# A prefix block of gated linear attention, Mamba-2 and PEER on one core: the opening products queued half a round earlier, a shorter look-ahead of the weight stream, and one step more in the first attention head

## The chip, the cores and the metric

The kernel runs on one core of one Trainium2 chip. The metric is device microseconds of one launch, from the first to the last instruction with what little lies around it; lower is better.

## The reference

One layer of a hybrid backbone. 256 latent tokens and 256 context tokens (512 columns together) of width D = 2048 pass through an RMSNorm that is modulated by the conditioning vector, one wide input projection that feeds gated linear attention (GLA, 4 heads) and a Mamba-2 state-space mixer, merge gates, an output projection, and then a second modulated norm and product-key experts (PEER).

```python
# modulation: six vectors of D for the latent tokens (from c) and for the context tokens (from c_ctx)
h = rmsnorm(x, w) * (1 + scale) + shift              # the same for ctx
q, k, v, r, lr_f, lr_b, z, xbc, dt_f, dt_b, gl = split(h @ w_in)
g_f = log_sigmoid(lr_f @ w_lr2_f + b_lr_f) / 16      # log decays of GLA, and g_b from lr_b
# GLA, a head: qd = q exp(b), kd = k exp(-b); o = tril(qd kd^T) v + qd s; both directions
...
# Mamba-2 SSD, merge gates, output projection, gated residual; then norm, PEER experts, gated residual
```

## The kernel before

All products are float32 to nearly full precision: each operand is split into a high and a low part, and a product is three matmuls (high by high, high by low, low by high). So every 512 KB chunk of weights (a tile `raw`, 128 x 1024) is split before TensorE uses it: ScalarE (ACT) copies it to `hi` (line 49), and VectorE (DVE) subtracts to get `lo` (line 50). The class `Stream` holds the list of chunks, loads them on SyncE's queue (line 42, three buffers `raw`) and splits them (four buffers each of `hi` and `lo`). `get()` hands the next chunk to the products, and first calls `ahead()`, which issues loads up to `loads` chunks ahead and splits up to `splits` ahead. Instructions run on each engine in the order in which the code issues them.

The same SyncE queue carries the weights of the modulation, called rides (line 64, 512 KB each, tiles `raw0` and `s4`, seven slots in the opening). Two rides feed one piece: `ada_piece` (line 263, tile `ad`, eight short matmuls in the trace). A ride's slot comes free when the piece has run on TensorE that used the ride seven before it. A load `raw` that has to wait for its buffer holds up the rides behind it in the queue.

The opening computes the modulated input `Hhi`, `Hlo` pair by pair of 128-row tiles, and the products that can begin with a part of it. A list `START`, written out by a loop over rounds, sets the order. A round has four pieces; after the fourth the sums stand in `ad`, and `ada_out` copies them (ACT, line 269), turns them (TensorE, line 274, `sc<-sel,s`) and adds the bias (DVE, line 279, `mods`). `h_pair` (lines 309 to 321) then makes one pair: DVE scales (line 314), ACT rounds to `Hhi` (line 316), DVE subtracts to `Hlo` (line 318), and DVE prepares the next pair (line 321). Each pair feeds two products `v` (`v_part`, lines 336 to 338, 12 matmuls into four banks `mm`) and two products `ld` (lines 426 to 428, 6 matmuls into banks `sc`); in the later rounds a whole product `k` follows (lines 328 to 330, 24 matmuls, a bank `sc`). There are 32 pieces, 8 turnings, 16 `v`, 16 `ld` and 4 `k` in the opening.

After it come the units, one weight tile after another (lines 328 to 330, banks `mm`), with the decays (`dt_stage` from line 665, `decay` lines 482 to 500) and the attention heads as generators beside them: at each `tick`, once per weight chunk, a generator runs up to its next `yield`. `gla(hd)` takes the exponentials of a head (`exps`, lines 534 to 550), multiplies (`prods`, lines 555 to 561) and multiplies on TensorE (`diag`, line 568).

The lines that the change touches are `START` and what reads it, `Stream._load` and `Stream._split`, the tag of the copy in `ada_out`, and two yields in `gla`.

Of the kernel before, what the change touches and what calls it, by code (L numbers as in the profile page):

```python
# [10 lines left out]
F32 = mybir.dt.float32  # L11
F32R = mybir.dt.float32r
# [7 lines left out]
P = 128  # L20
# [8 lines left out]
class Stream:  # L29
# [8 lines left out]
        self.rides, self.aboard, self.nr = [], deque(), 0  # L38

    def _load(self, i):  # L40
        t = self.pool.tile([P, 1024], F32, name="raw", tag="raw", bufs=self.loads - self.splits)
        self.nc.sync.dma_start(t, self.plan[i])
        self.raw[i] = t

    def _split(self, i):
        t = self.raw.pop(i)
        hi = self.pool.tile([P, 1024], F32R, name="hi", tag="hi", bufs=self.splits + 1)
        lo = self.pool.tile([P, 1024], F32R, name="lo", tag="lo", bufs=self.splits + 1)
        self.nc.scalar.activation(hi, t, AF.Copy)  # L49
        self.nc.vector.tensor_sub(lo, t, hi.bitcast(F32))  # L50
        self.done[i] = (hi, lo)
# [43 lines left out]
def hybrid_block_kernel(ctx, tc, A, out):  # L95
    nc = tc.nc
# [4 lines left out]
    streams = ctx.enter_context(tc.tile_pool(name="streams", bufs=1))  # L101
    dram = ctx.enter_context(tc.tile_pool(name="dram", bufs=1, space=DRAM))
    psum = ctx.enter_context(tc.tile_pool(name="psum", bufs=1, space=PSUM))
    st = Stream(nc, streams, 6, 3)

    def mmbank(shape=(P, 512)):
        return psum.tile(list(shape), F32, name="mm", tag="mm", bufs=4)
# [42 lines left out]

    START = []
    for c in range(10):
        todo = [("v", c - 2, 0), ("ld", c - 2, 0), ("v", c - 2, 1), ("ld", c - 2, 1)] if c > 1 else []
        if 4 < c < 9:
            todo.append(("k", c - 5, 0))
        for i in range(8):
            if c < 8 and i % 2:
                START.append(("ada", c, i // 2))  # L160
                if not c:
                    START.append(("norm", i // 2, 0))
            if i == 3 and 0 < c < 9:
                START.append(("h", c - 1, 0))
            if todo:
                START.append(todo.pop(0))

    plan = []
    for k, a, b in START:
        if k == "ada":  # L170
# [39 lines left out]
    w4 = es_w.enter_context(tc.tile_pool(name="w4", bufs=1, reuse_waits="tile"))  # L210
    es_x = ExitStack()
    xp = es_x.enter_context(tc.tile_pool(name="xp", bufs=1))
# [46 lines left out]
    def ada_piece(i, raws=None):  # L259

        raws = [r.rearrange("p (k n) -> p k n", k=2) for r in (raws or st.alight())]
        for g in range(4):
            mm_(adb[32 * g:32 * g + 32, :], cS[:, 4 * i + g, :], raws[g // 2][:, g % 2, :], start=i == 0, stop=i == 3,  # L263
                tile_position=(0, 32 * g), skip_group_check=True)
# [26 lines left out]
    def norm1():  # L291
        pst = scbank()
        for i in range(4):
            sq = [xp.tile([P, 512], F32, name="sq1", tag="sq1", bufs=3) for _ in range(2)]
            for j in range(4):
                nc.scalar.activation(sq[min(j, 1)], xc[:, 4 * i + j], AF.Square)
                if j:
                    nc.vector.tensor_add(sq[0], sq[0], sq[1])
            mm_(pst, ones, sq[0], start=i == 0, stop=i == 3)
            if i != 1:  # L300
                yield
        nc.scalar.activation(rs1, pst, AF.Ln, bias=eps, scale=1.0 / D)
        nc.scalar.activation(rs1, rs1, AF.Exp, scale=-0.5)
        nc.vector.tensor_mul(xc[:, 0:2], xc[:, 0:2], rs1[:, None, :].to_broadcast([P, 2, 512]))
        yield
# [37 lines left out]
    bg, later, ended = [], [], set()  # L343
# [3 lines left out]
    def step():  # L347
        todo = later[:]
        later.clear()
        for g in list(bg):  # L350
            if next(g, "end") == "end":
                bg.remove(g)
        for f in todo:
            f()
# [38 lines left out]
    XT, CT = slice(0, 256), slice(0, 512)  # L393
    pv0 = [mmbank() for _ in range(4)]
    n1 = norm1()
    ada_sb = lambda: w4.tile([P, 512], F32, name="s4", tag="s4", bufs=5)
    plr = pdt = None
    Kt = {a: w4.tile([P, 2, 512], F32, name="s4", tag="s4", bufs=5) for a in range(2)}
    for k, a, b in START:
        if k == "ada":  # L400
            ada_piece(b)
            if st.nr < start_rides:
                st.board()
            if b == 3:
                bg.append(ada_out(a))
        elif k == "norm":
            next(n1)
            if a == 3:
                st.ahead()
        elif k == "h":  # L410
            while ("ada", a) not in ended:
                step()
            h_pair(a)
        elif k == "v":
            if b == 0:
                wv = v_weights()
            v_part(pv0, wv, 2 * a + b, b)
        elif k == "ld":
            kt = 2 * a + b
            if kt == 0:  # L420
                plr, pdt = scbank(), scbank()
            if kt % 4 == 0:
                ld = [w.rearrange("p (w k f) -> p w k f", w=2, f=P) for w in st.get()]
            for w, pp in enumerate((plr, pdt)):
                Whi, Wlo = (t[:, w, kt % 4] for t in ld)
                mm_(pp, Whi, Hhi[:, kt, CT], start=kt == 0, stop=False)
                mm_(pp, Whi, Hlo[:, kt, CT], start=False, stop=False)
                mm_(pp, Wlo, Hhi[:, kt, CT], start=False, stop=kt == KT - 1)
        else:
            pk = scbank()  # L430
            mm3(pk, st.get(), 0, 8, Hhi, Hlo, CT, True, True)
            later.append(lambda a=a, pk=pk: nc.scalar.activation(Kt[a // 2][:, a % 2], pk, AF.Copy))
        step()
    es_x.close()
    wk = es_w.enter_context(tc.tile_pool(name="wk", bufs=1, reuse_waits="tile"))
    st.limit = st.side = None
    SZ = {"s1": 256, "s2": 512, "s4": 1024}
    NBUF = {"s1": 10, "s2": 22, "s4": 5}

    def wt(tag, shape, dtype=F32):  # L440
        assert int(np.prod(shape[1:])) <= SZ[tag]
        return (w4 if tag == "s4" else wk).tile(list(shape), dtype, name=tag, tag=tag, bufs=NBUF[tag])
# [79 lines left out]
    def gla(hd):  # L522
# [40 lines left out]
        def diag(d):  # L563
            qd, kd = E[d][1:3]
            for n in range(2):
                s = slice(n * P, n * P + P)
                for k in range(2):
                    mm_(P1[:, 2 * d + n], kd[:, k, s], qd[:, k, s], start=k == 0, stop=k == 1)
# [3 lines left out]
        prods(0)  # L572
        yield from exps(1)
        yield
        diag(0)
        prods(1)
        yield
        yield
        diag(1)
        P2 = scbank((P, 2, P))  # L580
        for d in range(2):
# [505 lines left out]
    for i in range(8):  # L1087
# [4 lines left out]
        t = mp.tile([P, 2, T], F32, name="ma", tag="mx", bufs=8)  # L1092
# [3 lines left out]
    for i in range(8):  # L1096
# [3 lines left out]
        t = op.tile([P, 2, 256], F32, name="mt", tag="mt", bufs=2)  # L1100
# [36 lines left out]
    for i in range(8):  # L1137
# [7 lines left out]
        for e in range(2):  # L1145
            k = 2 * i + e
# [198 lines left out]
    ada_sb = lambda: kp.tile([P, 512], F32, name="o2", tag="o2", bufs=3)  # L1345
    pq = {}
    for j, e, h in QORD:
        if j < 2:
            pq.setdefault((j, e), mmbank((P, 256)) if h == 0 else None)
        elif e == 0 and h == 0:  # L1350
            t = mmbank((P, 2, 256))
# [119 lines left out]
    for b in range(NB):  # L1471
# [4 lines left out]
        for group in ([0], [1], [2], [3]) if b < NB - 1 else ([0], [1], [2, 3]):  # L1476
# [7 lines left out]
            for order in ([(t, i, j) for i in group for j in range(2) for t in range(2)] if len(group) == 1 else  # L1484
                          [(t, i, j) for t in range(2) for i in group for j in range(2)]):
                t, i, j = order
# [96 lines left out]
```

## Time and profile before

| what | value |
|---|---|
| median of 3 runs | 3626.37 us (3626.19 to 3629.07) |
| profiled execution | 3628.86 us, span 3627.1 us |
| mean granted TensorE clock | 0.993 |
| TensorE matmul busy | 3546.5 us, 98% |
| VectorE, ScalarE, GpSimd busy | 65%, 46%, 10% |
| chain that ended last | PE 92%, DVE 4%, DMA 2%, ACT 1% |

The profiled execution lies 1.76 us above its span, and within the range of the three runs, 2.5 us above their median. TensorE is busy nearly all the time and makes up nearly all of the chain, so what is left to change is the 80 us in which it is not busy, and the stretches in which its clock is granted at the lower level.

### The profile page before, as it was taken

Reading aid. Unit: us, or ns where it says so; the run is one execution under the profiler, and the core shown is the slowest. Engines: PE = TensorE matmul, PEld = TensorE weight load, DVE = VectorE, ACT = ScalarE, POOL = GpSimd, SP = SyncE. Lnnn points to the kernel's source line nnn. Section 1 sums busy time; section 2 is a strip of 40 time slices with the busy share of each in tenths; the row PEclk is TensorE's granted clock in tenths of the full one; section 3 lists DMA queues with packets and bytes.
Section 4 is the critical chain, followed back from the end, with each engine's and each line's share of the span. In section 5 each row is a group of like instructions: output and inputs, shape, how many; then the busy total and the mean of one; then the engine's idle time right before and its main releaser. Section 6 shows DMA issues by size and latency. Waiting matters only on the chain.

```text
span 3627.1 us, 58908 instructions
## 1 busy us (share of the span) xinstructions
PE 3546.5 (98%) x23679; PEld 3186.4 (88%) x23679; DVE 2368.4 (65%) x3569; ACT 1665.6 (46%) x2225; POOL 370.6 (10%) x424
## 2 busy tenths in 40 slices
PE   5989999999999999999998999999999999999998
PEld 2688899988888888999998999999999999998886
DVE  3375565777878777655545787875555555556777
ACT  2254444445555555654433446464444444444344
POOL 0000000000000000110002016360000000000004
PEclk8999999999999999999999999999999999999999
DMA  8644555655665565567666557677666666666774
GB/s 304 230 140 142 172 170 179 208 170 189 210 206 184 176 191 174 167 230 245 193 209 218 172 182 203 195 208 221 198 198 197 198 197 198 198 198 206 240 228 144
DMA packets 214145, 715.39 MB, mean 197 GB/s; under 512 B 24688, under 2 KB 24832, under 8 KB 213360
## 3 DMA queue, kind: packets, MB, share of 16 engines
q1 hardware_dynamic: 188928, 625.04, 53.5%
q0 software_dynamic: 24944, 86.59, 8.7%
q8 instruction: 186, 3.05, 0.3%
q14 instruction: 87, 0.71, 0.1%
HBM read 679.93 MB, written 31.60 MB: 196 GB/s over the span
## 4 chain that ended last, share of the span: by engine, by line
PE 92%; DVE 4%; DMA 2%; ACT 1%; issue 1%; POOL 0%; DVEq 0%; SPq 0%; ACTq 0%; POOLq 0%
PE mm L328 20%; PE mm L330 20%; PE mm L329 19%; PE mm L1498 6%; PE mm L1497 6%; PE mm L1499 6%; PE mm L336 2%; PE sc L1304 2%; PE mm L337 2%; PE mm L338 2%; DVE lo L50 1%; PE sc L875 1%; PE ad L263 1%; PE sc L615 1%; PE sc L808 1%
## 5 line engine op out<-in xcount | busy, mean ns | idle before, releaser
L50 DVE TENSOR_TENSOR lo<-raw,hi 128x1024 fp32r<-128x1024 f32 x996 | 1234.3, 1246 | 1011.8 <-ACT hi L49 1003.5
L49 ACT ACTIVATE hi<-raw 128x1024 fp32r<-128x1024 f32 x996 | 1046.0, 1058 | 1383.5 <-PE mm L329 624.5
L328 PE MATMUL mm<-Hhi,hi 128*128 128x256 f32 (+1 forms) x2272 | 737.6, 325 | 1.4 <-ACT hi L49 1.4
L330 PE MATMUL mm<-Hhi,lo 128*128 128x256 f32 (+1 forms) x2272 | 724.7, 319 | 4.0 <-DVE lo L50 4.0
L329 PE MATMUL mm<-Hlo,hi 128*128 128x256 f32 (+1 forms) x2272 | 724.2, 319 | 0.0
L328 PE MATMUL mm<-h2hi,hi 128*128 128x256 f32 x2304 | 657.7, 285 | 0.0
L329 PE MATMUL mm<-h2lo,hi 128*128 128x256 f32 x2304 | 653.1, 283 | 2.5 <-DVE h2lo L1175 2.5
L330 PE MATMUL mm<-h2hi,lo 128*128 128x256 f32 x2304 | 652.6, 283 | 0.0
L328 PEld LDWEIGHTS mm<-Hhi,hi 128*128 128x128 f32 x2272 | 435.4, 192 | 37.0 <-issue 5.3
L330 PEld LDWEIGHTS mm<-Hhi,lo 128*128 128x128 f32 x2272 | 435.2, 192 | 34.4 <-DVE lo L50 5.0
L329 PEld LDWEIGHTS mm<-Hlo,hi 128*128 128x128 f32 x2272 | 435.7, 192 | 30.3 <-issue 1.9
L329 PEld LDWEIGHTS mm<-h2lo,hi 128*128 128x128 f32 x2304 | 442.4, 192 | 6.2 <-DVE h2lo L1175 3.1
L328 PEld LDWEIGHTS mm<-h2hi,hi 128*128 128x128 f32 x2304 | 442.1, 192 | 4.1 <-ACT h2hi L1172 0.8
L330 PEld LDWEIGHTS mm<-h2hi,lo 128*128 128x128 f32 x2304 | 442.1, 192 | 0.0
L1498 PE MATMUL mm<-lo,ph 128*128 128x512 f32 x1024 | 406.1, 397 | 5.7 <-DVE lo L50 5.7
L1497 PE MATMUL mm<-hi,ph 128*128 128x512 f32 x1024 | 406.5, 397 | 0.0
L1499 PE MATMUL mm<-hi,pl 128*128 128x512 f32 x1024 | 405.1, 396 | 0.0
L1498 PEld LDWEIGHTS mm<-lo,ph 128*128 128x128 f32 x1024 | 193.0, 188 | 49.5 <-DVE lo L50 7.2
L1499 PEld LDWEIGHTS mm<-hi,pl 128*128 128x128 f32 x1024 | 193.1, 189 | 46.3
L1497 PEld LDWEIGHTS mm<-hi,ph 128*128 128x128 f32 x1024 | 193.2, 189 | 42.8
L330 PE MATMUL mm<-yh,lo 128*128 128x256 f32 x768 | 217.3, 283 | 1.0 <-DVE lo L50 1.0
L328 PE MATMUL mm<-yh,hi 128*128 128x256 f32 x768 | 217.1, 283 | 0.0
(337 smaller groups left out, 4556.1 us busy)
## 6 DMA issues: line engine op xcount, KB each, us to landing
raw<-in_w_f_dram SPq DMA_DIRECT2D x288, 512.0 KB, 3.7
raw<-in_u_dram SPq DMA_DIRECT2D x256, 512.0 KB, 4.1
raw<-in_v_dram SPq DMA_DIRECT2D x256, 512.0 KB, 4.1
ride<-in_w_ada_dram SPq DMA_DIRECT2D x240, 256.0 KB, 3.9
raw<-in_w_so_dram SPq DMA_DIRECT2D x64, 512.0 KB, 4.2
raw<-in_w_ada_dram SPq DMA_DIRECT2D x45, 512.0 KB, 7.3
raw<-in_w_v_dram SPq DMA_DIRECT2D x32, 512.0 KB, 3.6
s<-cum_d POOLq DMA_DIRECT2D x64, 256.0 KB, 6.1
```

Of the source, the lines that this page charges most:

```text
L49: self.nc.scalar.activation(hi, t, AF.Copy)
L50: self.nc.vector.tensor_sub(lo, t, hi.bitcast(F32))
L328: mm_(ps, Whi[:, j, :], hi[:, k, tok], start=start and j == 0, stop=False)
L329: mm_(ps, Whi[:, j, :], lo[:, k, tok], start=False, stop=False)
L330: mm_(ps, Wlo[:, j, :], hi[:, k, tok], start=False, stop=stop and j == n - 1)
L336: mm_(pv[tb], Hhi[:, k, tok], Whi[:, j, :], start=k == 0, stop=False)
L337: mm_(pv[tb], Hhi[:, k, tok], Wlo[:, j, :], start=False, stop=False)
L338: mm_(pv[tb], Hlo[:, k, tok], Whi[:, j, :], start=False, stop=k == KT - 1)
L1304: mm_(pg[:, j], o1[:, j], o2[:, j], start=True, stop=True)
L1497: mm_(ps[t, i], ghi, Whi, start=j == 0 and k == 0, stop=False)
L1498: mm_(ps[t, i], ghi, Wlo, start=False, stop=False)
L1499: mm_(ps[t, i], glo, Whi, start=False, stop=j == 1 and k == 1)
```

## The change

Five edits, all in the first 280 us of the program.

1. `START`: a round has four slots instead of eight. The pair of round c - 1 is made right behind the first piece of round c, as before, but its products are queued from the third slot of the same round (before: from the first slot of the next round). Products stand one between two pieces, two where more than four are queued; what is left is put at the end, so that the last item is the last `k`.
2. `Stream(nc, streams, 5, 2)` in place of 6, 3 for the opening: loads run five chunks ahead and splits two. The numbers of buffers (three `raw`, four `hi` and `lo`), which were worked out from these two, are now written as they were. After the opening the look-ahead is set to 6, 3.
3. The copy of the sums takes a buffer `sq1` (three, used before that by the norm) instead of `s4`, a tag it shared with rides and the tiles of `k`.
4. After a `k` the loop goes on without a `step()`, and its copy (line 432) is issued behind the next item.
5. `gla(0)` yields once more ahead of `diag(0)` and once more ahead of `diag(1)`.

No instruction is added or removed on any engine; only the order changes, and in it only the opening and `gla(0)`.

```diff
     def _load(self, i):
-        t = self.pool.tile([P, 1024], F32, name="raw", tag="raw", bufs=self.loads - self.splits)
+        t = self.pool.tile([P, 1024], F32, name="raw", tag="raw", bufs=3)
...
-        hi = self.pool.tile([P, 1024], F32R, name="hi", tag="hi", bufs=self.splits + 1)
-        lo = self.pool.tile([P, 1024], F32R, name="lo", tag="lo", bufs=self.splits + 1)
+        hi = self.pool.tile([P, 1024], F32R, name="hi", tag="hi", bufs=4)
+        lo = self.pool.tile([P, 1024], F32R, name="lo", tag="lo", bufs=4)
...
-    st = Stream(nc, streams, 6, 3)
+    st = Stream(nc, streams, 5, 2)
...
-    START = []
+    START, todo = [], []
     for c in range(10):
-        todo = [("v", c - 2, 0), ("ld", c - 2, 0), ("v", c - 2, 1), ("ld", c - 2, 1)] if c > 1 else []
-        if 4 < c < 9:
-            todo.append(("k", c - 5, 0))
-        for i in range(8):
-            if c < 8 and i % 2:
-                START.append(("ada", c, i // 2))
-                if not c:
-                    START.append(("norm", i // 2, 0))
-            if i == 3 and 0 < c < 9:
+        for i in range(4):
+            if c < 8:
+                START.append(("ada", c, i))
+            if c == 0:
+                START.append(("norm", i, 0))
+            if i == 0 and 0 < c < 9:
                 START.append(("h", c - 1, 0))
-            if todo:
-                START.append(todo.pop(0))
+            if i == 2 and 0 < c < 9:
+                todo += [("v", c - 1, 0), ("ld", c - 1, 0), ("v", c - 1, 1), ("ld", c - 1, 1)]
+                if c > 4:
+                    todo.append(("k", c - 5, 0))
+            for _ in range(2 if len(todo) > 4 else 1):
+                if todo:
+                    START.append(todo.pop(0))
+    START += todo
...
-    ada_sb = lambda: w4.tile([P, 512], F32, name="s4", tag="s4", bufs=5)
+    ada_sb = lambda: xp.tile([P, 512], F32, name="sq1", tag="sq1", bufs=3)
...
             later.append(lambda a=a, pk=pk: nc.scalar.activation(Kt[a // 2][:, a % 2], pk, AF.Copy))
+            continue
+        while later:
+            later.pop(0)()
         step()
...
+    st.loads, st.splits = 6, 3
...
         yield from exps(1)
         yield
+        if hd == 0:
+            yield
         diag(0)
         prods(1)
         yield
         yield
+        if hd == 0:
+            yield
         diag(1)
```

TensorE around the first product, before. `ad` takes pieces (the last row that begins with `s4_` is the piece of two rides that were the first behind three loads), `mm` takes the first `v`:

```order
L263 MATMUL ad_147<-raw0_225,cS_143 32x512 x2
L263 MATMUL ad_147<-raw0_227,cS_143 32x512 x2
L263 MATMUL ad_147<-s4_256,cS_143 32x512 x2
L263 MATMUL ad_147<-s4_258,cS_143 32x512 x2
L336 MATMUL mm_150<-hi_240,Hhi_71 128x512
L337 MATMUL mm_150<-lo_241,Hhi_71 128x512
```

And after the change, the same place:

```order
L266 MATMUL ad_147<-raw0_225,cS_143 32x512 x2
L266 MATMUL ad_147<-raw0_227,cS_143 32x512 x2
L339 MATMUL mm_150<-hi_238,Hhi_71 128x512
...
L341 MATMUL mm_153<-hi_238,Hlo_72 128x512
L266 MATMUL ad_147<-s4_250,cS_143 32x512 x2
L266 MATMUL ad_147<-s4_252,cS_143 32x512 x2
L429 MATMUL sc_314<-Hhi_71,hi_242 128x512
...
L431 MATMUL sc_315<-Hhi_71,lo_243 128x512
L266 MATMUL ad_147<-raw0_274,cS_143 32x512 x2
L266 MATMUL ad_147<-raw0_276,cS_143 32x512 x2
L277 MATMUL sc_336<-sel2_108,sq1_312 128x2 x4
```

The first `v` (12 matmuls) now stands ahead of the piece that uses `s4_250` and `s4_252`, and one `ld` stands between that piece and the next.

VectorE between the norm and the first pair, before:

```order
L304 TENSOR_TENSOR xc_79<-xc_79,rs1_149 128x1024
L50 TENSOR_TENSOR lo_241<-raw_98,hi_240 128x1024
L50 TENSOR_TENSOR lo_245<-raw_100,hi_244 128x1024
L50 TENSOR_TENSOR lo_249<-raw_102,hi_248 128x1024
L279 TENSOR_TENSOR mods_142<-sc_260,b_ada_118 128x2x2x2
```

and after:

```order
L307 TENSOR_TENSOR xc_79<-xc_79,rs1_149 128x1024
L50 TENSOR_TENSOR lo_239<-raw_98,hi_238 128x1024
L50 TENSOR_TENSOR lo_243<-raw_100,hi_242 128x1024
L282 TENSOR_TENSOR mods_142<-sc_254,b_ada_118 128x2x2x2
```

One split fewer stands ahead of the first pair. On SyncE's queue the loads and rides of the same stretch stood, before, so:

```order
L42 DMA raw_234<-in_w_v_dram 128x1024
L42 DMA raw_236<-in_w_ld_dram 128x1024
L42 DMA raw_238<-in_w_v_dram 128x1024
L64 DMA s4_256<-in_w_ada0_dram 128x1024
L64 DMA s4_258<-in_w_ada0_dram 128x1024
```

and stand so after:

```order
L42 DMA raw_234<-in_w_v_dram 128x1024
L42 DMA raw_236<-in_w_ld_dram 128x1024
L64 DMA s4_250<-in_w_ada0_dram 128x1024
L64 DMA s4_252<-in_w_ada0_dram 128x1024
```

One load has left its place ahead of the two rides. In the first attention head TensorE went, before, from the last matmul of one chunk of a unit to `diag(0)` (line 568):

```order
L330 MATMUL mm_1671<-Hhi_71,lo_1572 128x256
L568 MATMUL sc_1556<-s2_1561,s2_1562 128x128 x4
L328 MATMUL mm_1671<-Hhi_71,hi_1624 128x256
```

and goes after (`diag` is now line 575):

```order
L333 MATMUL mm_1671<-Hhi_71,lo_1572 128x256
L331 MATMUL mm_1671<-Hhi_71,hi_1624 128x256
...
L333 MATMUL mm_1671<-Hhi_71,lo_1625 128x256
L575 MATMUL sc_1556<-s2_1561,s2_1562 128x128 x4
L331 MATMUL mm_1671<-Hhi_71,hi_1674 128x256
```

One chunk of 24 matmuls has moved ahead of `diag(0)`.

## Rows read from the trace of the kernel before

**Rows 1.** The page's busy times: us, share of the span, instructions.

```profile
PE 3546.5 (98%) x23679; PEld 3186.4 (88%) x23679; DVE 2368.4 (65%) x3569; ACT 1665.6 (46%) x2225; POOL 370.6 (10%) x424
```

**Rows 2.** Busy time of each engine in four stretches (us from the start): length, then PE, PEld, DVE, ACT, POOL busy with instructions, the granted TensorE clock, the DMA engines' share, GB/s.

```profile
20.00:30.00 10.00, 7.31 (x26) 1.42 (x22) 3.46 (x5) 4.20 (x8) 0.00 (x0) 0.93 1.03 420
40.00:90.00 50.00, 35.95 (x161) 18.36 (x162) 17.90 (x32) 8.05 (x13) 0.00 (x0) 0.83 0.75 276
94.70:185.60 90.90, 90.68 (x455) 61.88 (x454) 31.94 (x56) 22.40 (x31) 0.54 (x1) 1.00 0.57 211
196.00:235.00 39.00, 34.61 (x214) 31.71 (x214) 37.80 (x71) 18.95 (x28) 1.08 (x2) 0.94 0.38 97
```

**Rows 3.** TensorE in order of time, 38 to 95 us: start, duration, line, operation, and in brackets the idle time before it and what ended that.

```profile
38.06 1.93 PE L263 MATMUL ad<-raw,cS 128*32 128x512 f32 x16
48.88 3.13 PE L263 MATMUL ad<-s,cS 128*32 128x512 f32 x8 [8.90 <-DMA s<-in_w_ada_dram]
51.94 0.73 PE L336 MATMUL mm<-hi,Hhi 128*128 128x512 f32 x1
55.14 1.07 PE L263 MATMUL ad<-raw,cS 128*32 128x512 f32 x8
56.13 1.05 PE L274 MATMUL sc<-sel,s 128*128 128x2 f32 x8
57.05 0.48 PE L426 MATMUL sc<-Hhi,hi 128*128 128x512 f32 x1
...
73.10 0.63 PE L427 MATMUL sc<-Hlo,hi 128*128 128x512 f32 x1
73.53 0.63 PE L428 MATMUL sc<-Hhi,lo 128*128 128x512 f32 x1
...
86.13 1.51 PE L263 MATMUL ad<-raw,cS 128*32 128x512 f32 x4 [3.84 <-DMA raw<-in_w_ada_dram]
...
93.81 1.05 PE L274 MATMUL sc<-sel,s 128*128 128x2 f32 x8
```

**Rows 4.** SyncE's queue in order of time, 41 to 82 us: start, duration of the issues, line, tile from tensor.

```profile
41.95 0.33 SPq L42 DMA_DIRECT2D raw<-in_w_v_dram  x1
42.34 0.90 SPq L64 DMA_DIRECT2D s<-in_w_ada_dram  x2
...
56.34 0.39 SPq L64 DMA_DIRECT2D raw<-in_w_ada_dram  x1
63.81 0.33 SPq L42 DMA_DIRECT2D raw<-in_w_v_dram  x1
...
66.15 0.98 SPq L64 DMA_DIRECT2D s<-in_w_ada_dram  x2
81.07 0.33 SPq L42 DMA_DIRECT2D raw<-in_w_ld_dram  x1
```

**Rows 5.** Waits of SyncE's queue from 0 to 200 us: the waiting line, what released it, us in total, times, the longest.

```profile
SPq L42 <- DVE lo L50: 59.3, 12, 20.5
```

**Rows 6.** VectorE in order of time, 38 to 64 us.

```profile
38.44 3.49 DVE L50 TENSOR_TENSOR lo<-raw,hi 128x1024 fp32r<-128x1024 f32 x3
41.85 0.16 DVE L279 TENSOR_TENSOR mods<-sc,b_ada 128x8 f32<-128x8 f32 x1
...
43.67 1.34 DVE L318 TENSOR_TENSOR Hlo<-xc,Hhi 128x512 fp32r<-128x512 f32 x2
...
62.56 1.23 DVE L50 TENSOR_TENSOR lo<-raw,hi 128x1024 fp32r<-128x1024 f32 x1 [7.70 <-ACT hi L49]
63.70 0.16 DVE L279 TENSOR_TENSOR mods<-sc,b_ada 128x8 f32<-128x8 f32 x1
```

**Rows 7.** ScalarE in order of time, two rows between 43 and 80 us.

```profile
43.01 1.28 ACT L316 ACTIVATE Hhi<-xc 128x512 fp32r<-128x512 f32 x2 [2.90 <-DVE xc L314]
...
78.73 1.06 ACT L49 ACTIVATE hi<-raw 128x1024 fp32r<-128x1024 f32 x1 [12.10 <-PE mm L338]
```

**Rows 8.** TensorE where nothing waits, 172 to 182 us: the first matmul of a `k`, of the `v` after it, of the `ld` after that, and of the next `v`.

```profile
172.00 0.39 PE L328 MATMUL sc<-Hhi,hi 128*128 128x512 f32 x1
...
177.44 0.39 PE L336 MATMUL mm<-hi,Hhi 128*128 128x512 f32 x1
...
180.16 0.39 PE L426 MATMUL sc<-Hhi,hi 128*128 128x512 f32 x1
...
181.52 0.39 PE L336 MATMUL mm<-hi,Hhi 128*128 128x512 f32 x1
```

**Rows 9.** TensorE in order of time from the first unit to the first head's `diag`, 185 to 261 us.

```profile
185.60 0.39 PE L328 MATMUL mm<-Hhi,hi 128*128 128x512 f32 x1
...
201.94 0.50 PE L492 MATMUL sc<-lrS,s 128*128 128x512 f32 x1 [1.73 <-DVE s L487]
...
233.06 0.39 PE L330 MATMUL mm<-Hhi,lo 128*128 128x256 f32 x1 [2.18 <-DVE lo L50]
...
250.74 2.05 PE L568 MATMUL sc<-s,s 128*128 128x128 f32 x8 [3.78 <-DVE s L558]
...
259.79 1.13 PE L568 MATMUL sc<-s,s 128*128 128x128 f32 x8 [0.74 <-DVE s L558]
```

**Rows 10.** VectorE in order of time, 246 to 251 us.

```profile
246.96 1.23 DVE L50 TENSOR_TENSOR lo<-raw,hi 128x1024 fp32r<-128x1024 f32 x1 [3.71 <-PE mm L330]
...
249.90 0.69 DVE L558 TENSOR_TENSOR s<-s,s 128x512 f32<-128x512 f32 x1
```

## The prediction

> **What bounds the kernel now.** I read the page's busy times first, then the busy times by stretch, then the rows of each engine in the two stretches that the change touches. TensorE is busy for 98% of the span [rows 1], so a gain can come only from where it is not, or from where its clock is low. From 40 to 90 us it is busy for 35.95 of 50 us at a mean granted clock of 0.83; from 94.7 to 185.6 us it is busy for 90.68 of 90.9 us at 1.00 [rows 2]. The opening's loss thus lies almost all ahead of 95 us.
>
> To price that loss I put together what the opening would take with no wait. Undisturbed, a piece takes 0.99 us (55.14 to 56.13) and a turning of the sums 0.92 (56.13 to 57.05) [rows 3]; a `k` takes 5.44 us (172.00 to 177.44), a `v` 2.72 (to 180.16) and an `ld` 1.36 (to 181.52) [rows 8]. The pieces that start at 38.06 end at 39.99 [rows 3], and the first unit starts at 185.60 [rows 9], 145.6 us later. Between lie 25 pieces (24.8), 7 turnings (6.4), 16 `v` (43.5), 16 `ld` (21.8) and 4 `k` (21.8), 118.3 us. So 27.3 us are lost. Up to the end of the fourth turning (93.81 + 0.92 = 94.7 [rows 3]) there are 10 pieces, 3 turnings, 5 `v` and 4 `ld`, 31.7 us of work in 54.7 us: 23.0 us are lost there. The other 4.3 us come after it, where TensorE shows no idle time. They are the small delays where one kind of product follows another: the first `ld` matmul takes 0.48 us where the ones of a row take 0.39 [rows 3, 8].
>
> What makes the 23.0 us: TensorE waits 8.90 us for the first ride that stands behind three loads in SyncE's queue, runs that piece in 3.13 us in place of 0.99, and later waits 3.84 us for another ride; the matmuls around 73 us come 0.43 us apart where 2.72 us for a `v`'s twelve are 0.23, the lower of the clock's two levels, after the idle time ahead of them [rows 3]. Why the rides are late is seen on the queue. It stands still from 56.7 to 63.81 and from 67.1 to 81.07 us, each time in front of a load `raw` [rows 4], and such loads wait 59.3 us in all for the subtraction that frees their buffer [rows 5]. The subtraction waits for the copy `hi`, and that copy waited 12.10 us for a `v` on TensorE, the last reader of the `hi` buffer it was to fill [rows 7]. So the loop is: look-ahead of three splits with four buffers makes ScalarE wait for the product that runs, the load behind it waits, the rides behind the load wait, and TensorE waits for the rides.
>
> **The change part by part.** No instruction is added or removed; each term is a wait.
>
> *Look-ahead 5, 2.* With the same four buffers, a split goes into a buffer whose reader ended one chunk earlier, so the copy has no wait for the product that runs. This takes away the 12.10 us kind of wait on ScalarE and the two gaps in the queue, 7.1 and 14 us. It also takes one load out of its place ahead of the rides (41.95, [rows 4]) and one of three subtractions out of its place ahead of the first pair (38.44 for 3.49 us, so 1.15 us [rows 6]). What it costs: weights are split one chunk later. The cover is one chunk's product; between two chunks lie at least a `v` or `ld` and a piece, 2.35 us, against a copy (1.06) and a subtraction (1.23) in a row, 2.29 us [rows 6, 7], and mostly far more. I cost it at nothing.
>
> *Order of the products.* The first pair's `mods` come at 41.85, and its `Hhi` is whole at 43.01 + 1.28 = 44.3 [rows 6, 7]; 1.15 us earlier this is 43.1, the first of the two tiles about 42.5. In the new order the first `v` then runs while the ride for the next piece comes, instead of behind it. It starts cold: 12 matmuls at 0.43 are 5.2 us, to 47.7. The ride was issued at 42.34 [rows 4] and used at 48.88 [rows 3], 6.5 us; now it is issued about 41.2 with one transfer of 512 KB (0.524 MB at the 0.42 MB/us of 20 to 30 us [rows 2], 1.25 us) fewer ahead, so it lands by 46.5 to 47.7. The piece and that `v`, which ended at 55.1 before, end about 49.3: 5.8 us gained here. The work to there is 3.7 us of the 9.3 since 39.99, so 5.6 us stay lost.
>
> From there to the fourth turning the queue must bring 20 rides and 4 loads, 24 transfers or 12.6 MB, in the 39.7 to 80 us that a full TensorE gives them; a round needs 10 transfers, 5.2 MB, in 4 pieces, a turning, two `v` and two `ld`, 13.0 us. At the 420 GB/s of 20 to 30 us [rows 2] that is 12.5 us: just enough, so I leave 1.5 us of loss for it. The Trainium skill ("DMA: Bandwidth & Descriptors", section "Where 436 GB/s comes from") says that for transfers from HBM to SBUF the HBM side, about 358 GB/s, binds. By that a round would take 14.6 us, 1.6 us more than TensorE needs, some 6 us over four rounds, and the opening would gain 9 instead of the sum below; the 420 GB/s over ten microseconds of this trace speak against it.
>
> More changes of kind between products, two or so in a round, at 0.1 us each way as above: 1 us over the eight rounds gets worse. So the opening keeps 5.6 + 1.5 + 4.3 + 1.0 = 12.4 us of its 27.3 and gains 15. The bounds are 10 (one more wait like the 3.84 stays, with its slow matmuls) and 20 (the first `v` runs warm, the transfers never limit).
>
> *The tag of the sums' copy, the later copy of `k`.* The copy no longer waits for a ride's slot or a `k` tile. It must end ahead of the next piece, which now comes one `ld` (1.36 us) behind instead of one `v` (2.72); the copy has half the columns of a split's 1.06 us [rows 7], so some 0.5 us, and ScalarE is free then. Nothing; at worst, with a split (1.06) just ahead of it, 0.3 us in a round, 2.4.
>
> *The end of the opening.* The last `k` now stands between the last `v` and the first unit, so 5.44 us of TensorE's work lie over the emptying of the `v` banks and the first splits. In the units' first 40 us VectorE is busy 37.80 of 39.0 us [rows 2], and TensorE waits 1.73 us and 2.18 us for it [rows 9]. VectorE's work starts about 5 us earlier relative to TensorE's. Bounds: 0, as a full VectorE gives no time back, and the 3.9 of these two waits and some slow matmuls behind them, 6. I take 2.6.
>
> *`gla(0)`.* `diag(0)` waits 3.78 us for the multiplications, which end at 249.90 + 0.69 = 250.6 behind a subtraction that ended at 248.2; the matmuls after it are slow (2.05 us for eight, against 1.13 later) [rows 9, 10]. One chunk of 24 matmuls, 2.9 us, moves into the wait. Its `lo` is the subtraction that ended at 248.2, so it starts 1.2 us late. That leaves about 1.2 us of the 3.78, and takes away a part of the slow stretch (1 us). I take 3, bounds 0 (the same wait ahead of the chunk instead) and 5. The 0.74 of the second `diag` is left out.
>
> **The sum.** 15 + 2.6 + 3 = 20.6 us. From the profiled execution's 3628.9 that is 3608.3 us. That execution lies 2.5 us above the median of the runs shown, and the result will be a median, so I predict 3606.
>
> **The rivals.**
>
> *Only the opening gains.* VectorE, full from 196 to 235 us [rows 2], takes the end's gain back, and the chunk ahead of `diag(0)` waits for its own `lo` as long as `diag` waited. For it speaks that both are behind the same engine; against it, that in `gla(0)` the subtraction ended 2.4 us ahead of the products. 3626.4 - 15 = 3611.
>
> *The transfers bind.* If the queue delivers as from 40 to 90 us before, 276 GB/s [rows 2], the 12.6 MB take 45.6 us, so the fourth turning comes 5 us later than with 420, and the next round 19 in place of 13 us, 6 more. Of 15 us 4 are left; with 3 of the rest, 3619. Against it: those 276 hold two gaps of 7 and 14 us in which the queue itself waited for a buffer [rows 4].
>
> *Slower.* The cover of a pair got shorter. Between a turning and the first product of its pair stood an `ld`, `v`, `ld` and three pieces, 8.4 us; now a `v`, an `ld` and two pieces, 6.1 us. The pair itself takes 3.2 us (41.85 to 45.0 [rows 6]). Its bias add stood once 6.6 us behind its turning (57.05 to 63.70), since a subtraction that waited for its copy was ahead of it [rows 3, 6]. If that comes back in each round, a pair is 9.8 us behind, 3.7 us too late, with eight slow matmuls behind each (1.6 us): 7 times 5.3 is 37 us and the time 3643. It decides against the change from 2.9 us a round. Against it: the copy no longer waits for the product that runs, and so the subtraction doesn't.
>
> *The change doesn't do what it says.* The first ride stays as late and the queue finds another reason to wait: no more than the 5 of the first `v`, 3622 to 3626.
>
> **How the numbers follow.** Forecast (3602 to 3611) 0.50; more than that, down to 3597, 0.10; only the opening 0.15; transfers 0.13; no effect 0.07; slower 0.05. A change of 0.2%, 7.25 us, can be told from none: faster is below 3619.1, slower above 3633.6. Faster: 0.50 + 0.10 + 0.15 and half of the transfers, 0.82; slower 0.05; the rest 0.13. The range 3597 to 3619 leaves out no effect, slower, and the far half of the transfers, 0.18.
>
> **What would show it.** Right: the first `v` near 42.5 us and ahead of the piece; no gap over 5 us on SyncE's queue in front of a load between 50 and 90 us; no wait of `hi` on a `v` of 10 us; the fourth turning near 80 us and the first unit near 171; the wait ahead of `diag(0)` near 1 us. Wrong: TensorE waits for `Hhi` or `Hlo` in each round (the slower case), or for rides all through 50 to 90 us with the queue never standing still (transfers); or the first unit near 171 but the time at 3611 (only the opening).

## The result

The changed kernel takes 3605.99 us (median of 5 runs, 3605.44 to 3607.89) against 3626.19 (5 runs); the ratio is 0.9944, 95% interval 0.9932 to 0.9956. It is faster by 20 us, as forecast. The profiled executions lie further apart: their spans differ by 22.1 us, since the one before lies 2.7 us above its median. The changed kernel's profiled execution took 3606.86 us, with a span of 3605.0.

The page's busy times after, which answer to [rows 1]:

```profile
PE 3542.9 (98%) x23679; PEld 3183.0 (88%) x23679; DVE 2367.0 (66%) x3569; ACT 1666.1 (46%) x2225; POOL 372.0 (10%) x424
```

TensorE does the same matmuls, in 3.6 us less of busy time (the mean granted clock is 0.995 against 0.993); the other 18.5 us of the two spans were idle time. By stretch, to be read beside [rows 2]:

```profile
40.00:50.00 10.00, 7.47 (x24) 4.30 (x25) 5.74 (x11) 3.00 (x5) 0.00 (x0) 0.83 0.94 337
50.00:60.00 10.00, 10.00 (x58) 5.61 (x57) 6.55 (x11) 3.07 (x4) 0.00 (x0) 1.00 1.02 417
60.00:70.00 10.00, 10.00 (x59) 6.02 (x58) 3.11 (x9) 2.18 (x4) 0.00 (x0) 1.00 1.03 419
70.00:80.00 10.00, 10.00 (x59) 5.07 (x51) 3.38 (x3) 2.29 (x3) 0.00 (x0) 1.00 0.96 372
80.00:172.00 92.00, 92.00 (x465) 62.80 (x465) 38.05 (x65) 26.50 (x37) 0.54 (x1) 1.00 0.66 233
```

From 50 to 172 us TensorE is full at a granted clock of 1.00; its idle time in the opening, and its low clock, now lie from 40 to 50. TensorE in order of time there, with the first turning ahead of it, the fourth turning, and the first matmul of the first unit (compare [rows 3]):

```profile
36.78 1.05 PE L277 MATMUL sc<-sel,sq 128*128 128x2 f32 x8
37.77 1.92 PE L266 MATMUL ad<-raw,cS 128*32 128x512 f32 x16
42.27 0.79 PE L339 MATMUL mm<-hi,Hhi 128*128 128x512 f32 x1 [2.57 <-ACT Hhi L319]
...
46.87 1.05 PE L266 MATMUL ad<-s,cS 128*32 128x512 f32 x4
48.10 1.05 PE L266 MATMUL ad<-s,cS 128*32 128x512 f32 x4 [0.19 <-DMA s<-in_w_ada_dram]
49.09 0.50 PE L429 MATMUL sc<-Hhi,hi 128*128 128x512 f32 x1
...
51.67 1.05 PE L277 MATMUL sc<-sel,sq 128*128 128x2 f32 x8
...
79.67 1.05 PE L277 MATMUL sc<-sel,sq 128*128 128x2 f32 x8
...
169.40 0.39 PE L331 MATMUL mm<-Hhi,hi 128*128 128x512 f32 x1
```

The first turning stood in the kernel before at

```profile
37.07 1.05 PE L274 MATMUL sc<-sel,s 128*128 128x2 f32 x8
```

The first `v` runs at 42.27 while the ride comes, and the piece ends at 49.1. SyncE's queue in the same stretch (compare [rows 4]):

```profile
40.53 0.33 SPq L42 DMA_DIRECT2D raw<-in_w_ld_dram  x1
40.91 0.90 SPq L64 DMA_DIRECT2D s<-in_w_ada_dram  x2
...
52.03 0.33 SPq L42 DMA_DIRECT2D raw<-in_w_v_dram  x1
...
52.93 6.60 SPq L64 DMA_DIRECT2D raw<-in_w_ada_dram  x5
59.62 0.38 SPq L42 DMA_DIRECT2D raw<-in_w_ld_dram  x1
```

The two standstills of 7 and 14 us are gone. Up to 180 us the copy `hi` waited for a `v` like this before, and like this after (us in total, times, the longest):

```profile
ACT hi L49 <- PE mm L338: 37.9, 4, 12.1
```

```profile
ACT hi L49 <- PE mm L341: 1.9, 4, 0.5
```

The queue's loads, though, wait as long for the subtraction as in [rows 5] (59.3 us up to 200 us):

```profile
SPq L42 <- DVE lo L50: 63.7, 17, 10.8
```

So that total is no measure of the loss. Between 50 and 90 us no load holds the queue longer than the 4.8 us ahead of 52.03, and TensorE waits for no ride there.

Then the units. The first starts at 169.40 us, 16.2 earlier than in [rows 9]; rows from there to the next unit `v`, of which the last row is the seventh matmul, the first that waits for ScalarE to empty a bank:

```profile
183.15 0.43 PE L499 MATMUL sc<-lrS,s 128*128 128x512 f32 x1
...
208.89 0.38 PE L333 MATMUL mm<-Hhi,lo 128*128 128x256 f32 x1 [1.97 <-DVE lo L50]
...
214.20 0.39 PE L333 MATMUL mm<-Hhi,lo 128*128 128x256 f32 x1 [0.70 <-DVE lo L50]
...
228.20 0.39 PE L331 MATMUL mm<-Hhi,hi 128*128 128x256 f32 x1 [0.77 <-ACT hi L49]
229.46 0.39 PE L333 MATMUL mm<-Hhi,lo 128*128 128x256 f32 x1 [0.76 <-DVE lo L50]
233.69 1.05 PE L575 MATMUL sc<-s,s 128*128 128x128 f32 x8
...
258.01 0.50 PE L339 MATMUL mm<-hi,Hhi 128*128 128x512 f32 x1 [1.20 <-ACT s L981]
```

The first decay product no longer waits, nor does `diag(0)` (line 575); in its place two waits of 0.77 and 0.76 us stand at the chunk ahead of it. The two waits for `lo` near 209 and 214 us, 2.67 together, answer to waits of 0.48 (at 227.75) and 2.18 (at 233.06) before, so nothing was gained at these two. The row that answers to the last one stood in the kernel before at

```profile
279.84 0.51 PE L336 MATMUL mm<-hi,Hhi 128*128 128x512 f32 x1 [1.56 <-ACT s L970]
```

From the first unit to this row it took 94.2 us before and 88.6 after, 5.6 less. With the 16.2 of the opening that is 21.8 of the 22.1 us between the two spans; what comes later is as long as before.

### The profile page after: what moved, and what is told of

Same layout as the page of the kernel before. It is cut to its first block, busy times and chain, and to the rows that moved or that the text cites. A ratio compares the mean times of both kernels' runs of the same rounds, so it can differ in the third digit from the quotient of the medians.

```text
span 3605.0 us, 58893 instructions
## 1 busy us (share of the span) xinstructions
PE 3542.9 (98%) x23679; PEld 3183.0 (88%) x23679; DVE 2367.0 (66%) x3569; ACT 1666.1 (46%) x2225; POOL 372.0 (10%) x424
## 4 chain that ended last, share of the span: by engine, by line
PE 91%; DVE 4%; DMA 3%; ACT 1%; issue 1%; SPq 0%; DVEq 0%; POOL 0%; ACTq 0%; POOLq 0%
PE mm L331 19%; PE mm L332 19%; PE mm L333 19%; PE mm L1508 6%; PE mm L1509 6%; PE mm L1510 6%; PE mm L339 2%; PE sc L1315 2%; PE mm L340 2%; PE mm L341 2%; DVE lo L50 1%; PE sc L886 1%; PE ad L266 1%; PE sc L626 1%; PE sc L819 1%
```

## The experiments

All times are medians. Two measures of the trace tell more than the whole time: the first unit's start, and the time from there to the row of the `v` above, called the head below. What lies ahead of the second turning differs between executions: the first turning starts at 35.1 to 37.5 us, and in the five profiled executions that have the changed kernel's order and look-ahead up to there the second follows 14.6 to 16.9 us behind it. From the second turning to the first unit these five take 117.69 to 117.73 us. The opening of before was profiled twice, in the kernel before and with the yields alone, and took 148.5 and 145.8 us from the first turning to the first unit; from 70 to 80 us the granted clock was 0.83 in the one and 1.00 in the other.

**Look-ahead alone.** On the kernel before:

```diff
-    st = Stream(nc, streams, 6, 3)
+    st = Stream(nc, streams, 5, 2)
...
+    st.loads, st.splits = 6, 3
```

(with the buffers kept at three and four, and the second line behind the opening.)

> The kernel before with one edit: in the opening loads run five chunks ahead and splits two, with the same three and four buffers; order of the products, tag and attention as before. Theory (two halves: the look-ahead frees the queue, the order fills the first wait): the queue's two standstills in front of a load (7 and 14 us) and the 12 us wait of the copy hi on a v are gone, one load fewer stands ahead of the first ride, so the first wait shrinks from 8.9 to about 6.5 us and the 3.84 us wait and the slow matmuls after it go; of the 23.0 us lost up to the fourth turning about 11 stay, the fourth turning ends near 83 us in place of 94.7, the time is 3614 to 3617. Rival 1 (the order is all of it): the rides come as late as before, the fourth turning ends at 92 to 95, the time is 3622 to 3626. Rival 2 (the look-ahead is all of it): the same gain as the whole opening, the first unit starts near 169.5 to 171, the time is 3609 to 3611.

3612.8 us against 3627.8, ratio 0.9966 (0.9951 to 0.998). TensorE in order of time, and the waits of `hi` up to 180 us:

```profile
35.11 1.05 PE L274 MATMUL sc<-sel,s 128*128 128x2 f32 x8
...
46.09 3.17 PE L263 MATMUL ad<-s,cS 128*32 128x512 f32 x8 [7.98 <-DMA s<-in_w_ada_dram]
...
80.63 1.05 PE L274 MATMUL sc<-sel,s 128*128 128x2 f32 x8
...
170.23 0.39 PE L328 MATMUL mm<-Hhi,hi 128*128 128x512 f32 x1
...
186.78 0.50 PE L493 MATMUL sc<-lrS,s 128*128 128x512 f32 x1 [1.91 <-DVE s L488]
...
235.40 2.05 PE L569 MATMUL sc<-s,s 128*128 128x128 f32 x8 [4.54 <-DVE s L559]
```

```profile
ACT hi L49 <- PE mm L338: 5.4, 3, 1.8
```

The first wait is hardly smaller, and yet the fourth turning stands at 80.6 and the first unit at 170.2, 15.4 us earlier than before. Of these, 2.0 are an earlier first turning, within the scatter of that turning. From the first turning to the first unit it takes 135.1 us, against 148.5 before and 132.6 in the changed kernel: 13.4 of 15.9. The theory's half and half is wrong: in the opening the look-ahead is most of it, as rival 2 said, though the time lies 2 us above that rival's range. The waits of the units and the first head are as before.

**Look-ahead short at the first only.** The kernel of the last experiment, with the look-ahead of before set again at the first `v`:

```diff
+                if (a, b) == (0, 0):
+                    st.loads, st.splits = 6, 3
```

> The kernel before with the look-ahead of five and two only up to the first v, and of six and three from there on; order, tag and attention as before. One load fewer stands ahead of the first late ride and one subtraction fewer ahead of the first pair, as in the look-ahead alone; but from the first v on the copy hi again goes into the buffer whose reader is running. Theory (most of the look-ahead's 15 us comes from the copy that no longer waits for a running product, and so from the queue that no longer stands still): the standstills of 7 and 14 us are back, TensorE waits for rides again by the third or fourth turning, which ends near 91 us, the first unit starts at 181 to 185, and the time is 3622 to 3626. Rival (the one load and the one subtraction are it): the fourth turning ends at 81 to 84, the first unit starts at 170 to 174, and the time is 3611 to 3615.

3625.3 us, ratio 0.9999 (0.999 to 1.0008). SyncE's queue and TensorE:

```profile
55.82 0.33 SPq L64 DMA_DIRECT2D raw<-in_w_ada_dram  x1
63.43 0.33 SPq L42 DMA_DIRECT2D raw<-in_w_v_dram  x1
...
65.80 1.08 SPq L64 DMA_DIRECT2D s<-in_w_ada_dram  x2
78.85 0.33 SPq L42 DMA_DIRECT2D raw<-in_w_ld_dram  x1
```

```profile
83.72 3.62 PE L263 MATMUL ad<-raw,cS 128*32 128x512 f32 x8 [3.72 <-DMA raw<-in_w_ada_dram]
...
91.28 1.05 PE L274 MATMUL sc<-sel,s 128*128 128x2 f32 x8
```

The queue stands still for 7.3 and 12.0 us again, the copy `hi` waits 26.0 us for three `v` (the longest 9.9), the 3.7 us wait is back, the first unit starts at 183.6. So the gain comes from the copy that no longer waits for a running product, not from the one load and subtraction that left the front.

**Products half a round later.** The changed kernel, its products queued at the start of the next round:

```diff
-            if i == 2 and 0 < c < 9:
-                todo += [("v", c - 1, 0), ("ld", c - 1, 0), ("v", c - 1, 1), ("ld", c - 1, 1)]
-                if c > 4:
+            if i == 0 and 1 < c:
+                todo += [("v", c - 2, 0), ("ld", c - 2, 0), ("v", c - 2, 1), ("ld", c - 2, 1)]
+                if 4 < c < 9:
```

> The changed kernel with its products queued as before at the start of the next round (first v behind the second turning), all else as changed: round of four slots, look-ahead five and two, tag, attention. Theory (the first v fills the wait for the first ride): TensorE waits again for that ride, 7 to 8 us idle from 39.7 us with a cold piece behind it, and all later rounds run full; the first unit starts 4 to 6 us later than in the changed kernel (169.4), the time is 3610 to 3612. Rival (the queue sets the pace, so what TensorE does first doesn't matter): the first unit starts within 1 us of 169.4 and the time stays at 3606.

3616.1 us, ratio 0.9971 (0.9961 to 0.9981), the first unit at 178.7, 9.3 us later than in the changed kernel, where 4 to 6 were expected, and the time is 4 us above the theory's. One row of TensorE, and the busy times of a stretch:

```profile
46.85 3.16 PE L266 MATMUL ad<-s,cS 128*32 128x512 f32 x8 [8.03 <-DMA s<-in_w_ada_dram]
```

```profile
50.00:60.00 10.00, 9.30 (x39) 5.62 (x38) 5.40 (x11) 3.75 (x5) 0.00 (x0) 0.61 0.68 272
```

The wait of 8 us is back, and the clock, 0.61 in this stretch, stays low until near 58 us, inside the first `v`. That `v` starts at 54.30, behind the second turning, where in the kernel before it stood ahead of it: this list is later than the old one, so its loss overstates what the new list gains over the old. It also puts the last `k` back ahead of the last `v`, which adds to its head (92.5 us). So early queueing is worth at least the wait within the new rounds; beside the old list it is worth far less, since the look-ahead alone starts its units 8.5 us earlier than this kernel.

**The yields**, taken out of the changed kernel, and put alone into the kernel before:

```diff
-        if hd == 0:
-            yield
         diag(0)
...
-        if hd == 0:
-            yield
         diag(1)
```

> The changed kernel without the two added yields in the first attention head. Theory: the wait of 3.8 us in front of the first diag is back, with slow matmuls behind it; measured from the first unit's start (169.4) to the first v of the next unit, 88.6 us in the changed kernel, it takes about 3 us more, 91.6, and the time is 3609. Rival (the wait only moves from diag to the subtraction lo, as VectorE is full there): 88 to 89 us, and 3606.

> The kernel before with the two yields in the first attention head alone. Theory: from the first unit's start (185.6) to the first v of the next unit it took 94.2 us; the 3.78 us wait ahead of the first diag shrinks to about 1.2 and its slow matmuls go, 3 us less, 91.2, and the time is 3623. Rival (the wait only moves): 94, and 3626.

Without them 3611.1 us (3609 was expected), ratio 0.9959 (0.9945 to 0.9973), the head 91.4 us (2.8 more). Alone 3623.2, ratio 0.9990 (0.9980 to 1.0000), the head 91.0 us (3.3 less). TensorE in the one, and in the other:

```profile
232.48 1.50 PE L575 MATMUL sc<-s,s 128*128 128x128 f32 x8 [3.55 <-DVE s L565]
```

```profile
248.16 1.05 PE L568 MATMUL sc<-s,s 128*128 128x128 f32 x8
...
254.49 0.39 PE L330 MATMUL mm<-Hhi,lo 128*128 128x256 f32 x1 [0.76 <-DVE lo L50]
```

Both heads agree with the theory: the wait of `diag(0)` goes and comes with the yields, and smaller waits for splits take its place. Without the yields the whole time is 5.1 us above the changed kernel's 3606.0, 2.3 more than the head shows; where the rest comes from stays open.

**The last `k` ahead of the last `v`**, in the changed kernel:

```diff
+    i = START.index(("v", 7, 1))
+    START.insert(i, START.pop())
```

> The changed kernel with one item moved: the last k stands ahead of the last v and ld, as the items stood before, and not behind them. Theory (the last k covers the emptying of the v banks and gives VectorE a head start over the units): the first unit starts at 169.4 as in the changed kernel, but waits 0.4 us for its first lo and 1.7 to 1.9 us for the first decay product again with slow matmuls behind it; from the first unit to the first v of the next unit 88.6 becomes 91.5, and the time is 3609. Rival (the head start came from the shorter look-ahead or the later copy of k, not from where k stands): 88.6 and 3606.

3608.1 us, ratio 0.9945 (0.9929 to 0.9962); in the whole time that isn't told apart from the changed kernel. The head differs: 92.5 us against 88.6. (In the list of before the last `k` stood one `v` and one `ld` earlier still.) TensorE:

```profile
187.61 0.50 PE L501 MATMUL sc<-lrS,s 128*128 128x512 f32 x1 [1.80 <-DVE s L496]
...
218.75 0.53 PE L335 MATMUL mm<-Hhi,lo 128*128 128x256 f32 x1 [2.18 <-DVE lo L50]
```

The wait of the first decay product is back at its old size. The head start comes from where the last `k` stands, 3.9 us by this run.

**The tag.** In the changed kernel:

```diff
-    ada_sb = lambda: xp.tile([P, 512], F32, name="sq1", tag="sq1", bufs=3)
+    ada_sb = lambda: w4.tile([P, 512], F32, name="s4", tag="s4", bufs=5)
```

> The changed kernel with the copy of the sums back in the tag s4 that it shared with rides and the tiles of k. Theory (the tag is worth nothing): turnings and first unit within 0.5 us of the changed kernel (79.7, 169.4), time 3606. Rival (the copy waits for a ride's slot, or a ride for the copy's): turnings come later round by round, 1 us each, the first unit at 173 to 178 and the time at 3610 to 3614.

3605.6 us, ratio 0.9942 (0.9925 to 0.9958); fourth turning 79.9, first unit 169.6. No gain of the tag shows. The later copy of `k` was not run alone.

**Old rounds with the first `v` early.** The changed kernel with the loop of the old list in place of the new one, and three items moved behind it:

```diff
+    for item, after in ((("v", 0, 0), ("ada", 1, 2)), (("ld", 0, 0), ("ada", 1, 3)), (("k", 3, 0), START[-1])):
+        START.remove(item)
+        START.insert(START.index(after) + 1, item)
```

> The changed kernel with the list of before in its opening, except that the first v stands ahead of the piece whose rides come late, the first ld behind that piece, and the last k at the end; look-ahead, tag and attention as changed. With the look-ahead alone a round without k takes 13.57 us, in the changed kernel 14.0. Theory (new rounds change more often between pieces and products and lose 0.4 us a round; what the new order gives is the first v alone): the first unit starts 2 to 2.5 us earlier than in the changed kernel, near 167, the rest is as there, and the time is 3603 to 3604. Rival (rounds of 14.0 us are set by the transfers, not by the changes): the rounds get as long as in the changed kernel, the first unit starts at 169 to 170, and the time is 3606.

3606.6 us, ratio 0.9941 (0.9925 to 0.9958). The third and fourth turnings:

```profile
66.04 1.05 PE L277 MATMUL sc<-sel,sq 128*128 128x2 f32 x8
...
79.61 1.05 PE L277 MATMUL sc<-sel,sq 128*128 128x2 f32 x8
```

A round takes 13.57 us against the changed kernel's 14.00, so the transfers don't set its length. But from the second turning to the first unit, the same work in both, it gains 1.4 us (116.3 against 117.7), not 2 to 2.5, and in this execution the clock recovered 2 us later in the first stretch, which hid it. The time shows no difference.

**A look-ahead of four and one**, with these rounds and with those of the changed kernel, and the two beside the changed kernel on one chip:

```diff
-    st = Stream(nc, streams, 5, 2)
+    st = Stream(nc, streams, 4, 1)
```

> As old_rounds_first_v_early, with loads four chunks ahead and splits one in the opening. One subtraction fewer (1.15 us) stands ahead of the first pair and one load fewer ahead of the first late ride. Theory (what is left of the first loss is the wait for the first pair): the first v starts 1.1 us earlier, near 41.2, the piece behind it 1 us earlier, later rounds as long as there, and the time is 1 us less, 3602 to 3603. Rival (one split ahead is too few): TensorE waits for lo of a chunk just split, 1 to 2 us at each of the 12 chunks where only a short product stands between, the first unit starts 5 us or more later, and the time is 3608 or more.

> The changed kernel with loads four chunks ahead and splits one in its opening, nothing else. Theory (what is left of the first loss is the wait for the first pair, and in later rounds a split one chunk ahead is enough): first v at 41.0 or earlier against 42.3, from the second turning to the first unit 117.7 us as in the changed kernel, the time 1 to 2 us below it, 3604. Rival (with products one between two pieces, one split ahead is too few): TensorE waits for lo, the second turning to the first unit takes 120 or more, and the time is 3608 or more.

> The changed kernel as it is, beside the two others on one chip. 3606 by either theory; what is wanted is its distance to the two kernels with a look-ahead of four and one.

> The kernel old_rounds_first_v_early_lookahead_4_1 once more, beside the changed kernel on one chip. Theory (1.4 us from rounds with fewer changes between pieces and products, 1 to 2 from the first pair): 2 to 4 us below the changed kernel, 3602 to 3604. Rival (chance of single runs): within 1 us of it.

The old rounds gave 3602.2 us, ratio 0.9933 (0.9916 to 0.9949), and the second time 3604.0, 0.9937 (0.9923 to 0.9950); the changed rounds 3604.9, 0.9941 (0.9927 to 0.9954); the changed kernel again 3605.4, 0.9943 (0.9930 to 0.9957). TensorE in the changed rounds:

```profile
39.78 0.50 PE L339 MATMUL mm<-hi,Hhi 128*128 128x512 f32 x1 [1.32 <-ACT Hhi L319]
...
47.97 1.05 PE L277 MATMUL sc<-sel,sq 128*128 128x2 f32 x8
```

The first `v` waits 1.3 instead of 2.6 us, and in the changed rounds from the second turning to the first unit it takes 117.7 us, as in the changed kernel: one split ahead is enough. The three runs with four and one lie below the changed kernel, but the intervals overlap; whether the old rounds with four and one are better than the changed kernel by 1 to 4 us stays open.

The new order with the look-ahead of before (six, three) cannot run with four buffers of `hi`. Ahead of a `v`, ScalarE would get the copy of a chunk into a buffer that an `ld` still reads; this `ld` stands on TensorE behind a turning; and the turning waits for the copy of the sums, which in the new list stands on ScalarE behind that copy `hi`. Each waits for the next, so none can begin. Five buffers don't fit beside the rest of the opening. The gain of the order is therefore known on the shorter look-ahead only.

## Why the prediction was right

**The sum.** Predicted 15 for the opening, 2.6 for its end and 3 for the first head, 20.6 in all, 3606; measured 3605.99. From the first turning to the first unit the trace shows 132.6 us after and 148.5 before, 15.9 less, and 5.6 in the head, where 2.6 + 3 was forecast. Beside the other execution of the old opening (145.8) the opening's gain is 13.2, so the traces bear out the 15 no closer than this.

**The look-ahead.** Its mechanism held: no wait of `hi` on a running `v` above 0.5 us, no standstill of the queue of 5 us ahead of a load from 50 to 90 us, fourth turning at 79.7 (forecast near 80). It was costed at nothing, and TensorE waits for no split from 50 to 172 us. The experiment that goes back to the old look-ahead from the first `v` on loses the whole gain.

**The order of the products.** The steps came as worked out: first `v` at 42.3 (42.5), piece ended at 49.1 (49.3). The opening keeps 11.4 us of loss (129.7 us from 39.69 to 169.40, with 118.3 of work), where 12.4 was forecast: 5.7 up to 49.1 (5.6), and 5.7 behind it, where TensorE shows no idle time up to 172 us (1.5 + 4.3 + 1.0).

What was mis-sized is what the order is worth at the end. Beside the look-ahead alone, the changed kernel is 3.5 us ahead at the second turning (14.9 us behind the first, against 18.4) and has done one `ld` (1.36) more, so the order gains 4.9 us there. From the second turning to the first unit it needs 117.7 against 116.7, and that with the `ld` less to do, so it gives back 2.4, and 2.5 stay; with the scatter of the second turning that is 0.5 to 2.8. The failed term is the one for more changes of kind between products, 1 us over the eight rounds. It is 2.4 us by this comparison and 1.4 by the old rounds with the first `v` early; a round without `k` takes 14.00 against 13.57, 0.43 more. (The term's own factors, two changes of 0.1 us in eight rounds, make 1.6.) Of the 1.5 us for the transfers nothing shows, and that works the other way.

That leaves the look-ahead, for which the prediction had some 10 us (15, less 5.8 for the first `v`, plus the 1.0). It is 13.4 beside the profiled execution before and 10.7 beside the other one, so whether it was sized too low stays open. That the sum came out to the microsecond is in part chance: terms were wrong both ways, and the traces it is read from differ by more than that.

**The end of the opening.** 3.9 us by the run that moves the last `k` back, against 2.6, within the bounds of 0 to 6. The rival that VectorE gives it back is out: VectorE is as full as before (37.83 of the 39 us that answer to those of [rows 2]), but its first split of the units starts 5.7 us ahead of the first unit (163.70), where it was 0.3 (185.34).

**`gla(0)`.** 2.8 and 3.3 us by the two runs, against 3. The chunk ahead of `diag(0)` waits 0.77 + 0.76, forecast 1.2. End and head together are 5.6, less than 3.9 + 2.8: so the two gains don't add up in full. Waits for splits come in their place (0.77, 0.76 and 0.68 us near 228 to 239 us); that both rest on VectorE would explain it, but no run isolates that.

**The rivals.** The transfers didn't bind: TensorE waits for no ride from 48.1 to 172 us, with 417 and 419 GB/s from 50 to 70 us. The Trainium skill's limit of about 358 GB/s ("DMA: Bandwidth & Descriptors", section "Where 436 GB/s comes from") is exceeded by these rows for twenty microseconds; on this one core the measurement decides. In the slower case a pair would come late behind a subtraction; in this trace the bias adds of the second to fifth turnings stand 0.2 us behind the turnings' ends, and TensorE waits for `Hhi` once, at the first.

## What to carry to other kernels

When one in-order engine prepares buffers for another, look at whose reader it has to wait for: preparing one step less ahead with the same buffers took a wait out of ScalarE, the queue behind it and the engine behind that, and gave 11 to 13 us for two changed numbers. Moving work into a wait is worth the wait less what the new order costs in all the rounds where nothing waited; here about half of it was lost again. And a sum can be right while its terms trade places, so each edit should be run alone before its part is believed.

## What the runs showed of the hardware

512 KB transfers on one queue ran at 417 and 419 GB/s over two stretches of 10 us in which TensorE was full, with the DMA engines' share at 1.02 and 1.03.

Where the clock falls in the first stretch differs between executions of the same program. In the changed kernel the first `v` behind the 2.57 us wait ran at the low level (0.79 us for its first matmul); in the kernel with the last `k` moved, whose opening is the same up to there, that `v` began at the high level (0.50 us), and of the piece behind a later wait of 1.84 us the second half ran low (1.92 us for four matmuls, against 1.05 for the first four):

```profile
42.01 0.50 PE L341 MATMUL mm<-hi,Hhi 128*128 128x512 f32 x1 [2.57 <-ACT Hhi L321]
...
47.13 1.05 PE L268 MATMUL ad<-s,cS 128*32 128x512 f32 x4 [1.84 <-DMA s<-in_w_ada_dram]
48.40 1.92 PE L268 MATMUL ad<-s,cS 128*32 128x512 f32 x4 [0.22 <-DMA s<-in_w_ada_dram]
```

From the first to the second turning it takes 14.9 us in the one and 16.9 in the other. A single profile is no measure of a microsecond there.
